# Swapping the PSUM pairs of the seven products, and emitting two activation sums later, in a hybrid decoder trunk

## The chip, the cores and the metric

The kernel runs on one core of one Trainium2 chip. The metric is the device time of one execution in microseconds: before the change 1286.51 us, the median of 3 runs from 1285.29 to 1288.07. The profile is one further execution. Engines are called by the names that the profile uses: PE multiplies matrices (PEld is its load of the stationary operand), DVE, ACT and POOL work element by element, SP issues most DMAs.

## The reference

A sequence of 512 tokens with 1024 channels passes two layers. Layer 0 mixes tokens by stick-breaking attention with 16 heads, layer 1 by a gated linear recurrence with 8 heads. Each mixer is followed by a squared-ReLU MLP of width 4096, with an RMSNorm in front:

```python
def squared_relu_mlp(h, w1, w2):
    a = jax.nn.relu(h @ w1)
    return (a * a) @ w2
...
    h = rmsnorm(x, norm_gains[layer, 1])
    x = x + squared_relu_mlp(h, mlp_w1[layer], mlp_w2[layer])
```

Everything is float32. The change lies in the MLP alone, which runs twice.

## The kernel before

Every matrix product is made of three multiplications of a reduced format: both operands are split into a high and a low part (`xh`, `xl` for activations, `wh`, `wl` for weights), and high times high, high times low and low times high are added up in PSUM.

The MLP (`mlp`) runs in four rounds, q = 0 to 3, each for 1024 of the 4096 hidden features.

- The first half of a round makes the hidden features from four slabs of `mlp_w1`, c = 0 to 3. Each slab gives two tiles, j = 0 and 1, by `gemm_w`: a chain of 24 matmuls, 8 groups of 3, into one PSUM bank. In each group the second and the third matmul are (low activations, `wh`) and (high activations, `wl`). DVE then makes `u` from the bank (ReLU times the norm's factor, line 866), and `Seven.take` squares it and forms sums and differences of the halves of the activations.
- The second half multiplies by `mlp_w2` with Strassen's seven products (`seven_products`). They are named n = 0 to 6: a11, s1, a12, s4, s2, s3, a22. Each has its own slab of weights and two chains, t = 0 and 1, of 12 matmuls. After each chain a function (`p1` to `p7`) adds the bank to the residual stream `xt` on DVE, by `back` (line 714), some by way of a tile `U`.

PSUM has eight banks of 128x512: a pair called `mm`, a pair called `z`, three called `tr` and one called `av`. A pair is used in turn. The tiles of the first half use `mm` (in round 0 the first two use `z`). The products take `mm` for even n and `z` for odd n, so the first product (a11) and the last (a22) use `mm`, as do the hidden features ahead of a11 and behind a22. A chain can begin only when the bank has been read by whoever used it last.

The weights come through `Weights`. One call of `next` hands out the slab that is ready and prepares the one after it: SP or POOL load the raw half slabs, ACT makes `wh` (line 266 for `mlp_w1`, line 301 for `mlp_w2`), DVE makes `wl` (lines 267 and 302). Each slab has two halves, so there are two ACT and two DVE instructions per slab. There are two buffers for `wh`, `wl` and for the raw tiles `wr` of `mlp_w1`. The sums and differences of weights are made by DMAs that add on arrival, and by an ACT sign flip on line 293; its first flip for the next round is issued as soon as the data of the next round have landed.

PE runs in the order of the program. The other engines run in an order that a scheduler makes at build time from the order of the program and its own estimate of when each input is ready; every engine then works through its list in order.

`Seven.take` handles features 0 to 7 of a round. For features 4 to 7 (k = 0 to 3 after `k -= 4`) it makes `a2`, `s31` and, by two DVE subtractions on lines 785 and 786 and one more split, `s42`. `s42` is read by products n = 3 and n = 4.

Of the kernel before, what the change touches and what calls it, by code (L numbers as in the profile page):

```python
# [13 lines left out]
ALU = mybir.AluOpType  # L14
# [45 lines left out]
def trunk(  # L60
# [17 lines left out]
    nc = tc.nc  # L78
# [13 lines left out]
    def sb(tag, shape=(P, S), dt=F32, name=None):  # L92
        pool = gp if tag in "PQ" else ap
        return pool.tile(list(shape), dt, tag=tag, bufs=BUFS[tag], name=name or tag)

    def ps(tag, shape=(P, S), name=None):
        return pp.tile(list(shape), F32, tag=tag, bufs=PB[tag], name=name or f"ps_{tag}")

    def f(t):
        return t.bitcast(F32)  # L100
# [78 lines left out]
    def gain(layer, j, kt):  # L179
# [15 lines left out]
        out=later[:, 3 * P :], in_=later[:, 3 * P :], pattern=[[-1, P]], compare_op=ALU.is_gt,  # L195
# [4 lines left out]
        out=before[:, P:], in_=before[:, P:], pattern=[[1, P]], compare_op=ALU.is_gt,  # L200
# [188 lines left out]
    def gemm_w(o, wsl, j, acts, toks=slice(0, S)):  # L389

        hi, lo = wsl
        c = slice(j * P, (j + 1) * P)
        n = len(acts)
        for k in range(n):
            ah, al = acts[k]
            mm(o, hi[:, k, c], ah[:, toks], k == 0, False)
            mm(o, hi[:, k, c], al[:, toks], False, False)
            mm(o, lo[:, k, c], ah[:, toks], False, k == n - 1)
            yield
# [313 lines left out]
    def back(h, t, p, op=ALU.add):  # L713
        nc.vector.tensor_tensor(out=xt[h][:, t, :], in0=xt[h][:, t, :], in1=p, op=op)  # L714

    def chain(o, wsl, acts):

        hi, lo = wsl
        n = len(acts)
        for k, (ah, al) in enumerate(acts):  # L720
            mm(o, ah, hi[:, k, :], k == 0, False)
            mm(o, ah, lo[:, k, :], False, False)
            mm(o, al, hi[:, k, :], False, k == n - 1)
            yield
# [17 lines left out]
    def two(wsl, norm):  # L742

        got = [ps("z"), ps("z")]
        hi, lo = wsl
        for n, (h, task) in enumerate(norm.turned):
            yield [task]
            for j in range(2):
                c = slice(j * P, (j + 1) * P)
                for k in range(4 * h, 4 * h + 4):  # L750
                    ah, al = norm.acts[k]
                    mm(got[j], hi[:, k, c], ah, n == 0 and k == 4 * h, False)
                    mm(got[j], hi[:, k, c], al, False, False)
                    mm(got[j], lo[:, k, c], ah, False, n == 1 and k == 4 * h + 3)
                    yield
        return got

    class Seven:
# [5 lines left out]
        def take(self, u):  # L764

            A, B = slice(0, S // 2), slice(S // 2, S)
            k = len(self.raw)
            if k < 4:
                raw = sb("AT" if k else "qT", name="raw_a")
                self.raw.append(raw)  # L770
                nc.scalar.activation(out=raw, in_=u, func=AF.Square)
                hl = sb("Q", dt=F32R, name="a11")
                self.a11.append((hl[:, A], hl[:, B]))
                nc.scalar.copy(hl[:, A], raw[:, A])
                nc.vector.tensor_tensor(out=hl[:, B], in0=raw[:, A], in1=f(hl[:, A]), op=ALU.subtract)
                nc.vector.tensor_tensor(out=raw[:, A], in0=raw[:, A], in1=raw[:, B], op=ALU.subtract)
                return
            k -= 4
            a, raw = sb("sn", name="a"), self.raw[k]
            self.raw.append(a)  # L780
            nc.scalar.activation(out=a, in_=u, func=AF.Square)
            nc.vector.tensor_tensor(out=raw[:, B], in0=raw[:, B], in1=a[:, B], op=ALU.add)
            self.a2.append(self.two_parts(a, "Q", "a2"))
            self.s31.append(self.two_parts(raw, "qT", "s31"))
            nc.vector.tensor_tensor(out=a[:, B], in0=a[:, B], in1=raw[:, A], op=ALU.subtract)
            nc.vector.tensor_tensor(out=a[:, A], in0=a[:, A], in1=a[:, B], op=ALU.subtract)
            self.s42.append(self.two_parts(a, "Q" if k < 2 else "qT", "s42"))

        def two_parts(self, src, tag, name):
            h, l = act_pair(tag, name)  # L790
# [9 lines left out]
            }[name]  # L800
            return [[blk(x, at + t) for x in pair] for pair in src]

    def seven_products(A, done):


        U = []

        def p1(t, p):
            U.append(sb("AT", name="U"))
            nc.scalar.copy(U[t], p)  # L810
            back(0, t, p)

        def p2(t, p):
            back(0, t, p)
            done(0, t)

        def p5(t, p):
            back(1, t, p, ALU.subtract)
            back(1, 2 + t, p, ALU.subtract)

        def p3(t, p):
            back(1, t, p)

        def p6(t, p):
            nc.vector.tensor_add(U[t], U[t], p)  # L825
            back(1, t, U[t])
            done(1, t)

        def p7(t, p):
            nc.vector.tensor_add(U[t], U[t], p)  # L830
            back(1, 2 + t, U[t])
            done(1, 2 + t)
            back(0, 2 + t, U[t])

        def p4(t, p):
            back(0, 2 + t, p, ALU.subtract)
            done(0, 2 + t)

        steps = [
            ("a11", p1), ("s1", p5), ("a12", p2), ("s4", p3), ("s2", p6), ("s3", p7), ("a22", p4),  # L840
        ]
        for n, (name, then) in enumerate(steps):
            wsl = weights.next()
            for t in range(2):
                p = ps("z" if n % 2 else "mm", name="ps_mm")
                yield from chain(p, wsl, A.part(name, t))
                then(t, p)

    def mlp(norm, nxt=None):
        task = line.spawn(norm.finish())  # L850
        rounds = FF // D
        for q in range(rounds):
            A = Seven()
            for c in range(4):
                wsl = weights.next()
                if q + c == 0:
                    early = yield from two(wsl, norm)
                    yield [task]
                for j in range(2):
                    if q + c == 0:  # L860
                        p = early[j]
                    else:
                        p = ps("mm")
                        yield from gemm_w(p, wsl, j, norm.acts)
                    u = sb("sq", name="u")
                    nc.vector.scalar_tensor_tensor(  # L866
                        out=u, in0=p, scalar=0.0, in1=norm.R, op0=ALU.max, op1=ALU.mult
                    )
                    A.take(u)

            def done(h, t):
                if q < rounds - 1:
                    return
                if nxt is None:
                    nc.sync.dma_start(
                        out=out[0, t * P : (t + 1) * P, h * S : (h + 1) * S], in_=xt[h][:, t, :]
                    )
                    return
                nxt.squares(h, t)
                if t == TT - 1:  # L880
                    nxt.turn(h, LAG["x7"] if h else LAG["x"])

            yield from seven_products(A, done)


    def hgrn(norm):
# [274 lines left out]
    def trunk_steps():  # L1161
        outs, heads = yield from attention(Norm(0, 0))
        norm = Norm(0, 1)
        yield from project(outs, [heads[:8], heads[8:]], norm)
        nxt = Norm(1, 0)
        yield from mlp(norm, nxt)
        line.width = 3
        outs, mixes = yield from hgrn(nxt)
        norm = Norm(1, 1)
        yield from project(outs, [mixes[:4], mixes[4:]], norm)  # L1170
        yield from mlp(norm)
# [7 lines left out]
    for c in range(4):  # L1179
        for j in range(2):  # L1180
            k = 2 * c + j
            nc.sync.dma_start(
                out=xt[k // 4][:, :, (k % 4) * P : (k % 4 + 1) * P],
                in_=x[0, :, k * P : (k + 1) * P].rearrange("(t p) c -> p t c", p=P),
            )
            if j == 0:
                i = 2 * (c % 2)
                nc.sync.dma_start(
                    out=start["raws"][c // 2][:, i : i + 2, :],
# [10 lines left out]
    with tc.manual_schedule(engines={mybir.EngineType.PE}):  # L1200
        p = ps("av", name="ps_w")
# [52 lines left out]
```

## Time and profile before

| | before |
|---|---|
| median of 3 runs | 1286.51 us |
| the profiled execution's own time | 1282.32 us |
| its span | 1280.6 us |
| PE busy | 1241.3 us, 97% |
| DVE busy | 955.4 us, 75% |
| ACT busy | 611.1 us, 48% |
| PE waiting for `xt` on DVE in front of `ps_mm` | 5.0 us, 7 times |

The span is the time from the first to the last instruction in the trace; 1.7 us of the execution lie outside it. Matmuls of 512 columns start 0.23 us apart when nothing holds them up, but each is drawn 0.39 us long, since the next one starts while it is still under way. So the idle time that a row gives in front of a matmul is about 0.16 us less than the delay of its start.

### The profile page before, as it was taken

How to read it: one execution, taken by the hardware profiler on the slowest of the kernel's cores; microseconds unless marked ns; L12 is line 12 of the kernel's file. 1: busy time of each engine (PE TensorE's matmuls, PEld its weight loads, DVE VectorE, ACT ScalarE, POOL GpSimd, SP SyncE). 2: the span in 40 equal slices, each digit the busy share in tenths (PEclk: the TensorE clock that was granted, in tenths of full speed). 3: DMA queues.
4: the chain of work that ended last, by engine and by line, in shares of the span. 5: the costliest groups of instructions: out<-in, count | busy, mean ns of one | idle time of the engine just before them, and what ended most of it. 6: DMA issues, size and time to landing. Idle time of an engine off the chain costs nothing. (4 is left out here: it accounts for less than half of the span.)

```text
span 1280.6 us, 17916 instructions
## 1 busy us (share of the span) xinstructions
PE 1241.3 (97%) x6817; PEld 1071.3 (84%) x6817; DVE 955.4 (75%) x1799; ACT 611.1 (48%) x991; POOL 148.4 (12%) x207
## 2 busy tenths in 40 slices
PE   7999999999999999999999999999999999999998
PEld 7999999788878878788788888888888788787787
DVE  4798787865875866768878888888667758667686
ACT  4555455544734645536532424333346436356272
POOL 1000001000110100201022222223000101002010
PEclk8999999999999999999999999999999999999999
DMA  5312125332293572954321212225431944828615
GB/s 162 116 34 67 42 72 136 100 100 81 66 241 120 108 222 66 202 159 87 94 83 46 87 53 80 64 85 136 144 99 47 242 138 88 229 78 180 181 34 131
DMA packets 104502, 144.23 MB, mean 113 GB/s; under 512 B 4856, under 2 KB 70560, under 8 KB 104416
## 3 DMA queue, kind: packets, MB, share of 16 engines
q1 hardware_dynamic: 91024, 109.22, 26.6%
q0 software_dynamic: 13392, 33.87, 14.9%
q8 instruction: 54, 0.88, 0.3%
q14 instruction: 32, 0.26, 0.1%
HBM read 124.19 MB, written 2.10 MB: 99 GB/s over the span
## 5 line engine op out<-in xcount | busy, mean ns | idle before, releaser
L154 PE MATMUL ps_mm<-xh,wh 128*128 128x512 f32 x592 | 232.7, 393 | 4.0 <-DVE xt L714 4.0
L154 PE MATMUL ps_mm<-xh,wl 128*128 128x512 f32 x592 | 230.5, 389 | 0.0
L154 PE MATMUL ps_mm<-xl,wh 128*128 128x512 f32 x592 | 230.4, 389 | 0.0
L266 ACT CAST wh<-wr 128x1024 fp32r<-128x1024 f32 x134 | 136.8, 1052 | 143.3 <-PE ps_mm L154 87.0
L267 DVE TENSOR_TENSOR wl<-wr,wh 128x1024 fp32r<-128x1024 f32 x134 | 163.5, 1233 | 34.2 <-ACT wh L266 33.9
L154 PE MATMUL ps_mm<-wh,xh 128*128 128x256 f32 x592 | 172.8, 292 | 0.0
L154 PE MATMUL ps_mm<-wl,xh 128*128 128x256 f32 x592 | 167.5, 283 | 2.3 <-DVE wl L540 2.3
L154 PE MATMUL ps_mm<-wh,xl 128*128 128x256 f32 x592 | 167.7, 283 | 0.0
L302 DVE TENSOR_TENSOR wl<-raw,wh 128x1024 fp32r<-128x1024 f32 x112 | 132.8, 1221 | 35.9 <-ACT wh L301 35.8
L154 PEld LDWEIGHTS ps_mm<-xh,wh 128*128 128x128 f32 x592 | 111.2, 188 | 28.8 <-issue 6.4
L301 ACT CAST wh<-raw 128x1024 fp32r<-128x1024 f32 x112 | 111.4, 1047 | 43.9 <-PE ps_mm L154 40.4
L154 PEld LDWEIGHTS ps_mm<-xh,wl 128*128 128x128 f32 x592 | 111.1, 188 | 23.3
L154 PEld LDWEIGHTS ps_mm<-xl,wh 128*128 128x128 f32 x592 | 111.2, 188 | 22.2
L714 DVE TENSOR_TENSOR xt<-xt,ps_mm 128x512 f32<-128x512 f32 x128 | 86.1, 683 | 47.2 <-PE ps_mm L154 47.1
L154 PEld LDWEIGHTS ps_mm<-wl,xh 128*128 128x128 f32 x592 | 113.4, 191 | 3.0 <-DVE wl L540 2.5
L154 PEld LDWEIGHTS ps_mm<-wh,xh 128*128 128x128 f32 x592 | 113.4, 192 | 0.5
L154 PEld LDWEIGHTS ps_mm<-wh,xl 128*128 128x128 f32 x592 | 113.3, 191 | 0.0
L317 POOL DMA_DIRECT2D raw<-in_mlp_w_dram x16 | 19.4, 1242 | 585.0 <-DVE wl L302 585.0
L866 DVE SCALAR_TENSOR_TENSOR u<-ps_mm,R 128x512 f32<-128x512 f32 x60 | 41.3, 689 | 47.8 <-PE ps_mm L154 47.8
L293 ACT ACTIVATE raw<-raw 128x1024 f32<-128x1024 f32 x48 | 50.8, 1058 | 36.5 <-DMA raw<-in_mlp_w_dram 35.6
L1028 DVE COPY_PREDICATED sc<-masks,ps_s 128x32 f32<-128x32 uint8 (+9 forms) x176 | 46.6, 299 | 13.0 <-PE ps_s L154 11.0
L154 PE MATMUL ps_mm<-wl,s31h 128*128 128x512 f32 x128 | 51.2, 400 | 4.1 <-DVE wl L302 4.1
(236 smaller groups left out, 2547.9 us busy)
## 6 DMA issues: line engine op xcount, KB each, us to landing
raw<-in_mlp_w_dram SPq DMA_DIRECT2D x64, 512.0 KB, 5.9
wr<-in_mlp_w_dram SPq DMA_DIRECT2D x64, 512.0 KB, 4.2
raw<-in_mlp_w_dram POOLq DMA_DIRECT2D x32, 512.0 KB, 6.2
raw<-raw POOLq DMA_DIRECT2D x32, 512.0 KB, 5.8
wr<-in_hg_w_in_dram SPq DMA_DIRECT2D x32, 512.0 KB, 3.8
wr<-in_sb_w_qkv_dram SPq DMA_DIRECT2D x22, 512.0 KB, 3.5
wr<-in_sb_w_o_dram SPq DMA_DIRECT2D x8, 512.0 KB, 3.9
wr<-in_hg_w_o_dram SPq DMA_DIRECT2D x8, 512.0 KB, 4.1
```

Source lines behind the costliest of these rows:

```text
L154: nc.tensor.matmul(o, lhsT=lhsT, rhs=rhs, start=start, stop=stop, **kw)
L266: nc.scalar.copy(hi[:, c, :], raw)
L267: nc.vector.tensor_tensor(out=lo[:, c, :], in0=raw, in1=f(hi[:, c, :]), op=ALU.subtract)
L293: nc.scalar.mul(b[at][a], b[at][a], -1.0)
L301: nc.scalar.copy(hi[:, c, :], b[at][a])
L302: nc.vector.tensor_tensor(out=lo[:, c, :], in0=b[at][a], in1=f(hi[:, c, :]), op=ALU.subtract)
L317: nc.gpsimd.dma_start(out=b[0, 1][a], in_=rows(1, 1, a), accum_op=ALU.add)
L714: nc.vector.tensor_tensor(out=xt[h][:, t, :], in0=xt[h][:, t, :], in1=p, op=op)
L866: nc.vector.scalar_tensor_tensor(out=u, in0=p, scalar=0.0, in1=norm.R, op0=ALU.max, op1=ALU.mult)
L1028: nc.vector.copy_predicated(out=o, mask=mask.rearrange("p (g w) -> p g w", g=g)[:, None].to_broadcast([P, 2, g, w]), data=data.rearrange(" ...
```

## The change

The products of a round take the pairs the other way round (`z` for even n, `mm` for odd n), except in the last round (q = 3) of each MLP, which stays as it was. And of the last feature (k = 3) the two subtractions and the split into `s42` are no longer emitted inside `take` but in `seven_products`, right behind the call that hands out the slab of n = 0 and prepares that of n = 1.

```diff
@@ -782,9 +782,16 @@
             self.s31.append(self.two_parts(raw, "qT", "s31"))
-            nc.vector.tensor_tensor(out=a[:, B], in0=a[:, B], in1=raw[:, A], op=ALU.subtract)
-            nc.vector.tensor_tensor(out=a[:, A], in0=a[:, A], in1=a[:, B], op=ALU.subtract)
-            self.s42.append(self.two_parts(a, "Q" if k < 2 else "qT", "s42"))
+
+            def s42():
+                nc.vector.tensor_tensor(out=a[:, B], in0=a[:, B], in1=raw[:, A], op=ALU.subtract)
+                nc.vector.tensor_tensor(out=a[:, A], in0=a[:, A], in1=a[:, B], op=ALU.subtract)
+                self.s42.append(self.two_parts(a, "Q" if k < 2 else "qT", "s42"))
+
+            if k < 3:
+                s42()
+            else:
+                self.rest = s42
...
-    def seven_products(A, done):
+    def seven_products(A, done, last):
...
             wsl = weights.next()
+            if n == 0:
+                A.rest()
             for t in range(2):
-                p = ps("z" if n % 2 else "mm", name="ps_mm")
+                p = ps("z" if (n + (not last)) % 2 else "mm", name="ps_mm")
                 yield from chain(p, wsl, A.part(name, t))
                 then(t, p)
...
-            yield from seven_products(A, done)
+            yield from seven_products(A, done, q == rounds - 1)
```

No engine gets another instruction, and none loses one. What differs on PE is which matmuls wait, and for whom. At the end of round 0 of layer 0 PE has, before the change, the last matmul of a22 and then the first group of slab c = 0 of round 1 (`ps_mm_4099` is the bank of a22, t = 1; `ps_mm_4127` that of c = 0, j = 0; `wh_4075` and `wl_4076` are that slab):

```order
L154 MATMUL ps_mm_4099<-wh_4037,a2l_3828 128x512
L154 MATMUL ps_mm_4127<-xh_3321,wh_4075 128x512 [waits DVE_49,Activation_49]
L154 MATMUL ps_mm_4127<-xl_3322,wh_4075 128x512
L154 MATMUL ps_mm_4127<-xh_3321,wl_4076 128x512
L154 MATMUL ps_mm_4127<-xh_3337,wh_4075 128x512
```

And after it:

```order
L154 MATMUL ps_mm_4099<-wh_4037,a2l_3828 128x512
L154 MATMUL ps_mm_4127<-xh_3321,wh_4075 128x512 [waits DVE_49,Activation_49]
L154 MATMUL ps_mm_4127<-xl_3322,wh_4075 128x512
L154 MATMUL ps_mm_4127<-xh_3321,wl_4076 128x512 [waits DVE_49]
L154 MATMUL ps_mm_4127<-xh_3337,wh_4075 128x512
```

The first matmul still waits for a DVE instruction, now the one that read the bank two products earlier; the third has a wait of its own for the low half of the weights, which the first one's wait used to cover. The fifth group's third matmul has had a wait for the second half of `wl` in both.

Further up in the same round PE goes from c = 3 to a11 (n = 0). Before, with `ps_mm_3797` the bank of c = 3, j = 1, and `ps_mm_3853` that of a11, t = 0:

```order
L154 MATMUL ps_mm_3797<-xh_3496,wl_3650 128x512
L154 MATMUL ps_mm_3853<-wh_3747,a11_3553 128x512 [waits DVE_49,Activation_49]
L154 MATMUL ps_mm_3853<-wl_3748,a11_3553 128x512
L154 MATMUL ps_mm_3853<-wh_3747,a11_3553 128x512
L154 MATMUL ps_mm_3853<-wh_3747,a11_3561 128x512
```

After:

```order
L154 MATMUL ps_mm_3797<-xh_3496,wl_3650 128x512
L154 MATMUL ps_mm_3853<-wh_3747,a11_3553 128x512 [waits Activation_49]
L154 MATMUL ps_mm_3853<-wl_3748,a11_3553 128x512 [waits DVE_49]
L154 MATMUL ps_mm_3853<-wh_3747,a11_3553 128x512
L154 MATMUL ps_mm_3853<-wh_3747,a11_3561 128x512
```

The first matmul of a11 no longer waits for DVE to have read a bank of c = 3; the wait for `wl` has moved to the matmul that reads it.

On DVE the place is where the second slab of the products (n = 1, `wl` from `raw_3403` and `raw_3405`) meets the sums of the last feature (`a_3824`, `raw_a_3639`). Before:

```order
L866 SCALAR_TENSOR_TENSOR u_3822<-ps_mm_3797,R_3532 128x512 [waits PE_49]
L302 TENSOR_TENSOR wl_3842<-raw_3403,wh_3841 128x1024 [waits DMASW1_49,Activation_49]
L302 TENSOR_TENSOR wl_3842<-raw_3405,wh_3841 128x1024 [waits DMASW2_49,Activation_49]
L782 TENSOR_TENSOR raw_a_3639<-raw_a_3639,a_3824 128x256 [waits Activation_49]
L714 TENSOR_TENSOR xt0_99<-xt0_99,ps_mm_3853 128x512 [waits Activation_49]
L792 TENSOR_TENSOR a2l_3828<-a_3824,a2h_3827 128x512
L792 TENSOR_TENSOR s31l_3832<-raw_a_3639,s31h_3831 128x512 [waits Activation_49]
L785 TENSOR_TENSOR a_3824<-a_3824,raw_a_3639 128x256 [waits DVE_49]
L786 TENSOR_TENSOR a_3824<-a_3824 128x256 [waits DVE_49]
```

After:

```order
L875 SCALAR_TENSOR_TENSOR u_3822<-ps_mm_3797,R_3532 128x512 [waits PE_49]
L302 TENSOR_TENSOR wl_3836<-raw_3403,wh_3835 128x1024 [waits DMASW1_49,Activation_49]
L302 TENSOR_TENSOR wl_3836<-raw_3405,wh_3835 128x1024 [waits DMASW2_49,Activation_49]
L782 TENSOR_TENSOR raw_a_3639<-raw_a_3639,a_3824 128x256 [waits Activation_49]
L714 TENSOR_TENSOR xt0_99<-xt0_99,ps_mm_3853 128x512 [waits Activation_49]
L799 TENSOR_TENSOR a2l_3828<-a_3824,a2h_3827 128x512
L799 TENSOR_TENSOR s31l_3832<-raw_a_3639,s31h_3831 128x512 [waits Activation_49]
L787 TENSOR_TENSOR a_3824<-a_3824,raw_a_3639 128x256 [waits DVE_49]
L788 TENSOR_TENSOR a_3824<-a_3824 128x256 [waits DVE_49]
```

Nothing moved: the scheduler had put the second slab ahead of these sums already. Only line and buffer numbers differ. The same holds for the whole lists of DVE, ACT, POOL and SP, with their waits; on PE no matmul changes its place, and only the waits shown, in each of the six rounds that are not last ones, are others.

## Rows read from the trace of the kernel before

**Rows 1.** The page: busy time by engine, the granted PE clock in 40 equal slices of the span, and the chain that ended last by engine and by line.

```profile
PE 1241.3 (97%) x6817; PEld 1071.3 (84%) x6817; DVE 955.4 (75%) x1799; ACT 611.1 (48%) x991; POOL 148.4 (12%) x207
...
PEclk8999999999999999999999999999999999999999
...
PE 19%; DMA 3%; DVE 2%; issue 1%; ACT 0%; ACTq 0%; DVEq 0%
PE ps_mm L154 19%; DMA raw<-in_mlp_w_dram 3%; DVE wl L302 1%; DVE xt L714 1%; DVE U L825 0%; PE ps_z L154 0%; ACT wh L301 0%; DVE U L830 0%; PE ps_bc L154 0%; DVE dg L493 0%; DVE wl L267 0%; ACT raw L293 0%; ACTq L301 0%; DVEq L302 0%; ACTq L293 0%
```

**Rows 2.** The waits of PE over the whole span: who waited for whom, us in total, times, longest.

```profile
PE ps_mm L154 <- DVE xt L714: 5.0, 7, 1.0
PE ps_mm L154 <- DVE wl L302: 4.1, 6, 0.8
...
PE ps_mm L154 <- ACT wh L301: 1.1, 3, 0.6
```

**Rows 3.** The page's groups of instructions: the first matmul form of `gemm_w`, with the idle time in front of it, and the DVE additions into `xt` (count, busy us, mean ns).

```profile
L154 PE MATMUL ps_mm<-xh,wh 128*128 128x512 f32 x592 | 232.7, 393 | 4.0 <-DVE xt L714 4.0
...
L714 DVE TENSOR_TENSOR xt<-xt,ps_mm 128x512 f32<-128x512 f32 x128 | 86.1, 683 | 47.2 <-PE ps_mm L154 47.1
```

**Rows 4.** The timeline of PE where round 1 of layer 0 ends and round 2 begins: start us, duration us, then what ran, and in brackets the idle time before it and who ended it.

```profile
465.99 0.39 PE L154 MATMUL ps_mm<-wl,a2h 128*128 128x512 f32 x1
466.22 0.39 PE L154 MATMUL ps_mm<-wh,a2l 128*128 128x512 f32 x1
467.28 0.47 PE L154 MATMUL ps_mm<-xh,wh 128*128 128x512 f32 x1 [0.67 <-DVE xt L714]
467.58 0.40 PE L154 MATMUL ps_mm<-xl,wh 128*128 128x512 f32 x1
467.82 0.40 PE L154 MATMUL ps_mm<-xh,wl 128*128 128x512 f32 x1
468.05 0.40 PE L154 MATMUL ps_mm<-xh,wh 128*128 128x512 f32 x1
```

**Rows 5.** The loads of the stationary operand (PEld) for the first and the third matmul of the same group.

```profile
467.25 0.19 PEld L154 LDWEIGHTS ps_mm<-xh,wh 128*128 128x128 f32 x1 [1.06 <-issue]
...
467.59 0.19 PEld L154 LDWEIGHTS ps_mm<-xh,wl 128*128 128x128 f32 x1
```

**Rows 6.** The timeline of DVE over the same boundary.

```profile
463.39 0.68 DVE L830 TENSOR_TENSOR U<-U,ps_mm 128x512 f32<-128x512 f32 x1
464.11 1.29 DVE L714 TENSOR_TENSOR xt<-xt,U 128x512 f32<-128x512 f32 x2
465.32 1.22 DVE L267 TENSOR_TENSOR wl<-wr,wh 128x1024 fp32r<-128x1024 f32 x1
466.45 0.68 DVE L714 TENSOR_TENSOR xt<-xt,ps_mm 128x512 f32<-128x512 f32 x1
467.05 1.22 DVE L267 TENSOR_TENSOR wl<-wr,wh 128x1024 fp32r<-128x1024 f32 x1
468.18 0.68 DVE L714 TENSOR_TENSOR xt<-xt,ps_mm 128x512 f32<-128x512 f32 x1
471.38 1.23 DVE L267 TENSOR_TENSOR wl<-wr,wh 128x1024 fp32r<-128x1024 f32 x1 [2.51 <-ACT wh L266]
474.02 1.22 DVE L267 TENSOR_TENSOR wl<-wr,wh 128x1024 fp32r<-128x1024 f32 x1 [1.41 <-ACT wh L266]
```

**Rows 7.** The timeline of PE at the other five ends of a round that is not a last one: the first matmul of the next round.

```profile
382.36 0.47 PE L154 MATMUL ps_mm<-xh,wh 128*128 128x512 f32 x1 [0.69 <-DVE xt L714]
...
551.13 0.47 PE L154 MATMUL ps_mm<-xh,wh 128*128 128x512 f32 x1 [0.67 <-DVE xt L714]
...
1025.95 0.47 PE L154 MATMUL ps_mm<-xh,wh 128*128 128x512 f32 x1 [0.69 <-DVE xt L714]
...
1110.62 0.47 PE L154 MATMUL ps_mm<-xh,wh 128*128 128x512 f32 x1 [0.65 <-DVE xt L714]
...
1194.46 0.47 PE L154 MATMUL ps_mm<-xh,wh 128*128 128x512 f32 x1 [0.67 <-DVE xt L714]
```

**Rows 8.** The timeline of PE inside c = 0, j = 0 of round 2: the second and the third matmul of the fifth group, of which the third waits for the second half of `wl`; and, below, the first matmul of c = 1.

```profile
470.35 0.39 PE L154 MATMUL ps_mm<-xl,wh 128*128 128x512 f32 x1
470.58 0.39 PE L154 MATMUL ps_mm<-xh,wl 128*128 128x512 f32 x1
...
478.28 0.39 PE L154 MATMUL ps_mm<-xh,wh 128*128 128x512 f32 x1
```

**Rows 9.** The timeline of PE at the start of product s3 (n = 5) of round 1 of layer 0, and that of ACT ahead of it.

```profile
454.29 0.51 PE L154 MATMUL ps_mm<-wh,s31h 128*128 128x512 f32 x1 [0.57 <-ACT wh L301]
455.55 0.50 PE L154 MATMUL ps_mm<-wl,s31h 128*128 128x512 f32 x1 [0.75 <-DVE wl L302]
455.89 0.39 PE L154 MATMUL ps_mm<-wh,s31l 128*128 128x512 f32 x1
...
442.69 2.01 ACT L301 CAST wh<-raw 128x1024 fp32r<-128x1024 f32 x2 [3.45 <-PE ps_mm L154]
449.66 1.06 ACT L293 ACTIVATE raw<-raw 128x1024 f32<-128x1024 f32 x1 [4.96 <-DMA raw<-in_mlp_w_dram]
452.24 1.06 ACT L293 ACTIVATE raw<-raw 128x1024 f32<-128x1024 f32 x1 [1.52 <-DMA raw<-in_mlp_w_dram]
453.20 3.87 ACT L301 CAST wh<-raw 128x1024 fp32r<-128x1024 f32 x4
```

## The prediction

> **What bounds the kernel now.** Read the page first [rows 1]. PE is busy for 1241.3 of 1280.6 us, and the chain that ended last is PE's, with a few per cent of DVE and DMA. DVE is busy for three quarters of the span. So a change can pay only by what PE waits, some 39 us in all. The granted clock is 9 tenths or more, its upper level of 2.4 GHz, in every slice but the first, so none of these short waits costs clock.
>
> Next the waits of PE [rows 2]. Three of them belong to the MLP rounds: 5.0 us in 7 waits for the addition into `xt`, 4.1 us in 6 for `wl` of line 302, 1.1 us in 3 for `wh` of line 301. The groups [rows 3] show that 4.0 of the 5.0 us stand in front of the first matmul of `gemm_w`, that is, where one round follows another. Two layers with four rounds have six such places. The timelines show all six [rows 4, 7], with idle times of 0.65 to 0.69 us, always ended by the addition on line 714.
>
> Rows 4 to 6 tell why. PE is through with a22 and wants the pair `mm` for c = 0 of the next round. That pair still holds a22. Its first bank was full a chain ago, but DVE works through a list: the last addition of s3, then half of the next slab's `wl`, and only at 466.45 the addition that reads the bank. It ends at 467.13, and PE goes on at 467.28.
>
> **The stall that goes.** Undisturbed matmuls start 0.23 us apart. Here the start of c = 0 comes 467.28 - 466.22 = 1.06 us after the last matmul of a22, so it is 0.83 us late (the 0.67 us of the row and the 0.16 us by which a matmul is drawn longer than its spacing). The next start comes after 0.30 instead of 0.23 us, another 0.07. Together 0.90 us per place. Over six places: 4.0 us of idle time [rows 3], 6 x 0.16 = 1.0 and 6 x 0.07 = 0.4 make 5.4 us.
>
> After the change a22 sits in `z`, and c = 0 takes the `mm` banks of s3. DVE read the second of them at 463.39 to 464.07 (line 830) and the first before it [rows 6], over 2 us before PE asks at 466.45. So the bank no longer holds PE up. The next user of `z` is a11 of the next round, four slabs later, or in a last round s1.
>
> **What is late next.** Three things must be ready when PE starts at 466.45 instead of 467.28.
> - `wh` of the slab: ACT has long cast it.
> - The first half of `wl`. The order shows that the third matmul now waits for it by itself. It would start at 466.45 + 2 x 0.23 = 466.91. DVE ends this half at 465.32 + 1.22 = 466.54, and from a DVE end to PE's next step it takes 0.12 us (467.13 to the load at 467.25) [rows 5, 6], so it is there at 466.66. It fits with 0.25 us to spare. The second half ends at 468.27; the fifteenth matmul needs it at 466.45 + 14 x 0.23 = 469.7.
> - The slab of c = 1. Its last half of `wl` ends at 474.02 + 1.22 = 475.24 [rows 6]. PE began c = 1 at 478.28 [rows 8] and would begin it at 477.4. Two microseconds of cover stay; were they gone, the whole gain of that place would go with them.
>
> A wait that is already fulfilled costs nothing: the third matmul of the fifth group carries one today and starts 0.23 us after its neighbour [rows 8].
>
> The load of the stationary operand runs ahead: for the third matmul it started at 467.59, 0.23 us before the matmul at 467.82 [rows 4, 5]. The Trainium skill (TensorE: Matmul & The Clock Gate, "Step-by-step: what each phase is for") has the rule: PE pulls loads of weights ahead of matmuls that are under way. By it the new wait bites one matmul earlier, at 466.68 against a half slab that is there at 466.66, and the spare time is nothing; the trace agrees on the order of the two.
>
> What such a near miss costs is bounded by [rows 9]: where PE did stop for `wl`, the next start came after 0.34 instead of 0.23 us. A load that starts 0.1 us late still lets its matmul start on time (0.03 us behind it at 467.28, rows 4, 5), so the bounds are nothing and 0.11 us at each of six places, 0.7 us in all. I take 0.2 us, nearer to nothing, because the half slab is there on time by the rows.
>
> **The other edits.** The transition from c = 3 to a11 loses a wait for DVE that did not hold PE up: the waits of PE have no row of `u` in front of `ps_mm` among the MLP's [rows 2]. Worth nothing; a gain is excluded by the missing row, and a loss since the pair `z` has been free since the round before. The moved sums of the last feature keep their places in every list: the scheduler had placed the second slab's split ahead of them. Worth nothing, both ways, unless the lists differ on the chip, which they cannot.
>
> **The sum.** 5.4 - 0.2 = 5.2 us less. The profiled execution would go from 1282.32 to 1277.1 us, its span from 1280.6 to 1275.4. The median of the runs is 4.2 us above that execution; I take the difference off the median: 1286.5 - 5.2 = 1281.3 us.
>
> **Rivals.**
> 1. *The time is given back at product s3.* In rounds 0 to 2 PE waits there, 0.57 and 0.75 us by the rows shown, for a slab whose cast stands on ACT behind the sign flips of line 293, and these wait for data that SP and DMA bring [rows 9]. If the landing at 452.24 hangs on something that does not come earlier with PE, the stop grows by as much as PE gained. That takes back the gain of the four places that are followed by a round with this stop (into q = 1 and q = 2 in both layers), and leaves the two into q = 3, whose rounds have no such stop (6 waits in 8 rounds, rows 2): 2 x 0.9 = 1.8 us, 1284.7 us. For it speaks that DMA holds 3% of the chain. Against it: the cast at 442.69 is released by PE giving back a `wh` buffer, and raw buffers come free by the DVE instruction behind such casts, so this whole train starts when PE is at the products of the same round and moves with it.
> 2. *Slower: the new wait covers too much.* If the third matmul's wait on DVE came true only with the second half of `wl`, at 468.27 + 0.12 = 468.39, it would start at 468.4 instead of today's 467.82, and lose 0.58 and 0.1 for starting up again, 0.7 us at six places: 4.1 us, 1290.6 us. It decides as soon as that count is reached later than 0.9 us behind the first half. Against it: the fifth group keeps a wait of its own for the second half.
> 3. *The change does not do what it says.* Something else that DVE makes at the same moment would hold PE until 467.3 anyway, and the time stays 1286.5 us. The only inputs of the first two matmuls are old activations and `wh`, so I see nothing that could.
>
> **How the numbers follow.** A measurement of this kernel can tell about 0.2%, 2.6 us, from no change. Forecast 0.82 (5.2 us, 0.4%: faster), rival 1 0.09 (within 0.2%), rival 3 0.05 (within), rival 2 0.04 (slower). One in ten of the forecast's share may be spoilt by the spread of the runs, which reaches 1.6 us above the median, but then half of rival 1 may look faster. So faster 0.83, same 0.13, slower 0.04. The forecast's own range is a gain of 4.7 to 5.4 us, and 1 to 2 us on either side for the runs' spread and for the stops at s3, which differ between rounds by several tenths. Rival 1's 1284.7 us is taken in, rivals 2 and 3 are left out: 1278.5 to 1285.0 us.
>
> **What would show it.** Right: the waits of PE for `xt` in front of `ps_mm` fall from 7 to 1 and from 5.0 to about 1.0 us; the first matmul of each round starts 0.23 us after the last of a22; the waits for line 302 and line 301 keep their size. Rival 1: these two grow from 5.2 us together to about 9. Rival 2: a new wait of PE for `wl` of line 267, some 1.5 us each, six times. A few tenths of that row would be the near miss that I priced at 0.2. Wrong altogether would be the forecast if the first matmul of a round still stood idle, whoever ended it, or if DVE's additions at the boundary came later than now because a product's bank is read in another order.

## The result, and the profile after

| | before | after |
|---|---|---|
| median, runs on the same chip (5 each) | 1286.23 us | 1277.82 us |
| lowest to highest of them | 1281.2 to 1288.07 | 1275.55 to 1280.56 |
| the profiled execution's own time | 1282.32 us | 1279.44 us |
| its span | 1280.6 us | 1277.7 us |

The ratio is 0.9943, 95% interval [0.9921, 0.9966]: faster by 0.6%. That is about 8 us by the medians, 7.3 by the ratio, where 5.2 had been forecast. The two profiled executions differ by 2.9 us only. Both distances need an explanation, and the traces give most of it.

The page of the changed kernel, with the lines that answer to [rows 1] and the first of [rows 3]:

```profile
PE 1241.9 (97%) x6817; PEld 1073.6 (84%) x6817; DVE 955.0 (75%) x1799; ACT 611.8 (48%) x991; POOL 148.5 (12%) x207
...
PE 21%; DMA 2%; DVE 1%; ACT 0%; issue 0%; ACTq 0%
...
L154 PE MATMUL ps_mm<-xh,wh 128*128 128x512 f32 x592 | 232.1, 392 | 0.0
```

No engine works less or more. What changed is the last number: the idle time in front of the first matmul form of `gemm_w` was 4.0 us [rows 3] and is 0.0. The waits of PE (total us, times, longest) say the same:

```profile
PE ps_mm L154 <- DVE wl L302: 3.7, 6, 0.8
...
PE ps_mm L154 <- ACT wh L301: 1.7, 3, 0.9
...
PE ps_mm L154 <- DVE xt L714: 1.4, 2, 1.0
```

The wait for the addition into `xt` fell from 5.0 us in 7 times to 1.4 in 2; the two waits at s3 together went from 5.2 to 5.4 us [rows 2]. No row for `wl` of line 267 in front of `ps_mm` has appeared.

The timeline of PE where round 1 of layer 0 ends, which answers to [rows 4]:

```profile
466.11 0.39 PE L154 MATMUL ps_mm<-wh,a2l 128*128 128x512 f32 x1
466.33 0.39 PE L154 MATMUL ps_mm<-xh,wh 128*128 128x512 f32 x1
466.56 0.39 PE L154 MATMUL ps_mm<-xl,wh 128*128 128x512 f32 x1
466.79 0.39 PE L154 MATMUL ps_mm<-xh,wl 128*128 128x512 f32 x1
```

The load of the stationary operand for the third of these matmuls [rows 5]:

```profile
466.56 0.19 PEld L154 LDWEIGHTS ps_mm<-xh,wl 128*128 128x128 f32 x1
```

And DVE over the same boundary [rows 6]:

```profile
463.97 1.29 DVE L714 TENSOR_TENSOR xt<-xt,U 128x512 f32<-128x512 f32 x2
465.18 1.22 DVE L267 TENSOR_TENSOR wl<-wr,wh 128x1024 fp32r<-128x1024 f32 x1
466.32 0.68 DVE L714 TENSOR_TENSOR xt<-xt,ps_mm 128x512 f32<-128x512 f32 x1
```

DVE does what it did, in the same order and as late: its addition for a22 begins at 466.32. But PE passes from a22 to c = 0 in 0.23 us (466.11 to 466.33) where it took 1.06. The half slab of `wl` ends at 465.18 + 1.22 = 466.40, and the load that needs it starts on time at 466.56. All six round ends look like this: from the last matmul of a22 to the first of c = 1 it takes 11.11 us at every one, and took 12.03 to 12.08. That is 0.92 to 0.97 us six times, 5.7 us.

Why then do the profiled executions differ by 2.9 us? The trace of after has two stretches in which TensorE ran at its lower level of 1.2 GHz at places where the trace of before has none. When the two traces are matched matmul by matmul, after loses 2.4 us at each of these two places. Before has such a stretch of its own in layer 0's attention, at 239.7 to 243.1, which after lacks; there after gains 1.0 us. It gains 5.7 us at the round ends and 0.9 us at the start and in small waits, and all this together makes the 2.9 us. One of the two stretches is at s3 of round 0 of layer 0. PE's rows there:

```profile
367.57 0.40 PE L154 MATMUL ps_mm<-wh,s42l 128*128 128x512 f32 x1
368.83 0.50 PE L154 MATMUL ps_mm<-wh,s31h 128*128 128x512 f32 x1 [0.86 <-ACT wh L301]
370.09 0.61 PE L154 MATMUL ps_mm<-wl,s31h 128*128 128x512 f32 x1 [0.76 <-DVE wl L302]
370.50 0.63 PE L154 MATMUL ps_mm<-wh,s31l 128*128 128x512 f32 x1
370.93 0.63 PE L154 MATMUL ps_mm<-wh,s31h 128*128 128x512 f32 x1
```

And three windows of the same trace (window, its length, busy time and count of PE, PEld, DVE, ACT and POOL, then the granted clock, DMA share, GB/s): ahead of the stops, behind them, and later. The last line is the stretch in the trace of before.

```profile
366.50:367.50 1.00, 1.00 (x6) 0.82 (x5) 0.00 (x0) 0.75 (x2) 0.67 (x1) 1.00 0.93 356
370.50:373.50 3.00, 3.00 (x9) 2.33 (x8) 2.93 (x5) 1.11 (x2) 0.00 (x0) 0.50 1.09 198
380.00:383.00 3.00, 3.00 (x15) 2.47 (x14) 3.00 (x4) 0.00 (x0) 0.00 (x0) 1.00 0.31 85
```

```profile
239.70:243.10 3.40, 3.40 (x13) 2.63 (x12) 3.10 (x6) 0.67 (x2) 0.00 (x0) 0.50 0.01 2
```

After two stops in a row the granted clock is 0.50 for some 3 us; matmuls start 0.43 us apart instead of 0.23, eight of them, which is 1.6 us lost on top of the stops. The second such stretch stands behind two stops between the layers, at 640. From the start of the last matmul on `s42` to that of the first of a22, with the 24 of s3 between, it takes 9.50 us here and 7.10 in the trace of before; undisturbed it takes 5.82. (This is the segment at s3 that is meant below.) So one profiled execution more or less says little about a difference of 5 us; the segments between fixed instructions do.

### The profile page after: what moved, and what is told of

It is laid out like the page before. It is cut to its first block, busy times and chain, and to the rows that moved or that the text cites. A ratio compares the mean times of both kernels' runs of the same rounds, so it can differ in the third digit from the quotient of the medians.

```text
span 1277.7 us, 17916 instructions
## 1 busy us (share of the span) xinstructions
PE 1241.9 (97%) x6817; PEld 1073.6 (84%) x6817; DVE 955.0 (75%) x1799; ACT 611.8 (48%) x991; POOL 148.5 (12%) x207
## 5 line engine op out<-in xcount | busy, mean ns | idle before, releaser
L302 DVE TENSOR_TENSOR wl<-raw,wh 128x1024 fp32r<-128x1024 f32 x112 | 132.8, 1221 | 36.2 <-ACT wh L301 36.1
```

What stands on the lines that cost most here:

```text
L302: nc.vector.tensor_tensor(out=lo[:, c, :], in0=b[at][a], in1=f(hi[:, c, :]), op=ALU.subtract)
```

## The experiments

The ratios are to the kernel before, from runs on the same chip, with the 95% interval.

| run | kernel | median us | ratio |
|---|---|---|---|
| e1 | before, pairs swapped | 1278.66 | 0.9958 [0.9942, 0.9975] |
| e2 | before, sums moved | 1283.77 | 0.9997 [0.9985, 1.0009] |
| e3 | before, one DVE instruction more ahead of the round end | 1287.48 | 1.0027 [1.0016, 1.0037] |
| e4 | after, the same instruction | 1281.54 | 0.9980 [0.9969, 0.9991] |
| e5 | after, a quarter of it | 1278.51 | 0.9957 [0.9942, 0.9972] |
| e6 | after, swapped in last rounds too | 1279.60 | 0.9964 [0.9951, 0.9977] |
| e7 | after, a sign flip on POOL | 1279.94 | 0.9966 [0.9954, 0.9979] |
| e8 | after, that flip on POOL from round 1 on | 1270.03 | 0.9889 [0.9874, 0.9904] |
| e9 | after, again | 1277.08 | 0.9940 [0.9928, 0.9953] |
| e10 | before, with the flip as in e8 | 1271.00 | 0.9909 [0.9892, 0.9927] |
| e11 | before, again | 1284.95 | 1.0007 [0.9996, 1.0018] |

**The two parts, one at a time.** e1 is the kernel before with

```diff
-                p = ps("z" if n % 2 else "mm", name="ps_mm")
+                p = ps("z" if (n + (not last)) % 2 else "mm", name="ps_mm")
```

> Only the pairs are swapped; the last feature's sums stay where they were in the code. Theory (the banks do it all, the moved sums nothing): the same time as the changed kernel, ratio to the kernel before 0.993 to 0.997; PE's wait for xt in front of ps_mm 1 to 1.5 us. Rival (the part of the 8.4 us gain above the 5.2 us forecast comes from the moved sums): ratio 0.996 to 0.998, about 3 us above the changed kernel. Second theory, on the spread: the runs of one kernel differ by the number of 3.41 us stretches at half the granted clock; two runs whose mean clock differs by 0.0013 (one stretch more) differ by 1.5 to 2.1 us, and among runs of equal clock this kernel is 5 to 6 us ahead of the kernel before.

e2 is the changed kernel with that line put back, so that only the moved sums remain.

> Only the last feature's sums are emitted later; the pairs stay as before. Theory: nothing moves in any engine's list, so the kernel before: ratio 0.998 to 1.002, and PE waits 5 us for xt in front of ps_mm, six times 0.65 to 0.7 at the ends of rounds. Rival (the moved sums bring some 3 us): ratio 0.997 to 0.998.

e1's round ends are those of after (11.11 us, six times), e2's those of before but for one. In the waits of PE of e2 the row stands again:

```profile
PE ps_mm L154 <- DVE xt L714: 4.7, 7, 1.0
```

The banks do all of it; the sums do nothing. The one exception in e2 is a round end of layer 1 (at 1113.84) with 0.23 us: 12 us ahead of it the clock had fallen, PE was slower by that, and DVE had caught up before PE asked for the bank. With the old pairs, a stretch at the lower clock is thus partly hidden by the stall it shortens.

Of e1's second theory one half held: at equal clock e1's runs are 5.4 us ahead of those of the kernel before. The other half did not: by a straight line through these 35 runs, 0.0013 of mean clock goes with some 0.8 us, not 1.5 to 2.1.

**Is it DVE's lateness that sets the price?** e3 adds, in rounds that are not last, one DVE instruction without use right behind the second chain of s3, to the kernel with the old pairs; e4 adds it to the changed kernel:

```diff
         def p7(t, p):
             nc.vector.tensor_add(U[t], U[t], p)
+            if t == 1 and not last:
+                nc.vector.tensor_tensor(out=later[:, :S], in0=U[t][:, :S], in1=later[:, :S], op=ALU.max)
             back(1, 2 + t, U[t])
```

> The kernel before, with one more DVE instruction of 0.69 us ahead of the last additions of s3 in the six rounds that are not last ones; it adds work and leaves nothing out. Theory (PE waits for the bank that the addition on line 714 frees): every stop at a round's end grows by 0.69 us, PE's wait for xt from 5.0 to 9.1 us, the time by 4.1 us, ratio about 1.003. Rival (something else holds PE at that place): no change of the stop.

> The changed kernel with the same 0.69 us DVE instruction at the same six places. Theory (the bank no longer binds, the low half of the slab binds next, and its wait sits on the load of the stationary operand): the half slab is there at 0.65 us after the load wants it, the third matmul starts 0.45 us late and the one behind it another 0.1; 0.55 us at six places, 3.3 us above the changed kernel, PE waits about 3 us for wl of line 267. Rival 1 (DVE at that place no longer matters to PE): as the changed kernel. Rival 2 (a late load delays its matmul in full): 4 us or more above the changed kernel.

e5 is e4 with `:P` (128 columns) in place of `:S` (512).

> The changed kernel with a DVE instruction of 128 columns (0.2 to 0.3 us) ahead of the last additions of s3 in the six rounds that are not last ones; it adds work and leaves nothing out. It uses up what the half slab of wl has to spare. Theory (a load that comes late by less than its lead of 0.23 us costs nothing): the load of the third matmul waits 0.1 to 0.2 us, its matmul starts at most 0.05 us late, ratio to the kernel before as for the changed kernel, 0.9945 to 0.9965, PE waits under 0.5 us in all for wl of line 267. Rival (the wait counts from the load on, so its delay is passed on): 0.2 to 0.3 us at each of six places, 1.5 us above the changed kernel.

In e3 the wait grows to

```profile
PE ps_mm L154 <- DVE xt L714: 9.0, 8, 1.3
```

and the round ends from 1.04 to 1.08 us to 1.64 to 1.66, by 0.59: the added instruction is drawn 0.69 us long, but the next DVE instruction starts 0.61 behind it. In e4 the bank is not what PE waits for. It is the third matmul, for the half slab of `wl`; first PE's rows, then the load's, then DVE's:

```profile
468.23 0.39 PE L154 MATMUL ps_mm<-xh,wh 128*128 128x512 f32 x1
468.46 0.39 PE L154 MATMUL ps_mm<-xl,wh 128*128 128x512 f32 x1
468.97 0.50 PE L154 MATMUL ps_mm<-xh,wl 128*128 128x512 f32 x1
```

```profile
468.97 0.19 PEld L154 LDWEIGHTS ps_mm<-xh,wl 128*128 128x128 f32 x1 [0.55 <-DVE wl L267]
```

```profile
465.88 0.69 DVE L839 TENSOR_TENSOR later<-U,later 128x512 f32<-128x512 f32 x1
...
467.70 1.22 DVE L267 TENSOR_TENSOR wl<-wr,wh 128x1024 fp32r<-128x1024 f32 x1
```

The idle time is in the load's row, and the matmul's shows none, since 0.39 of the 0.51 us from its neighbour's start count as busy: that the start comes 0.28 us late is the sign. DVE was late by 0.62 us (465.88 to 466.50, where its next instruction starts), the load by 0.51 (it belongs at 468.46, with the matmul ahead of its own), the matmul by 0.28. Five of six segments went from 11.11 to 11.51 or more, by 0.44 us in the mean: the 0.28 us and some 0.15 until starts are 0.23 us apart again. The sixth followed a stretch at the lower clock and lost nothing. In e5 DVE was late by 0.21 us, and the segments took 11.11 to 11.15. PE and its loads where round 1 of layer 0 ends:

```profile
469.25 0.39 PE L154 MATMUL ps_mm<-xl,wh 128*128 128x512 f32 x1
469.48 0.40 PE L154 MATMUL ps_mm<-xh,wl 128*128 128x512 f32 x1
...
469.38 0.19 PEld L154 LDWEIGHTS ps_mm<-xh,wl 128*128 128x128 f32 x1 [0.16 <-DVE wl L267]
```

The load is 0.13 us late and its matmul on time, and no segment lost more than 0.05 us. So the spare is 0.1 us at the load and 0.3 us at the matmul; what goes beyond the second costs PE time.

**The exception for last rounds.** e6 drops it:

```diff
-                p = ps("z" if (n + (not last)) % 2 else "mm", name="ps_mm")
+                p = ps("z" if (n + 1) % 2 else "mm", name="ps_mm")
```

> The pairs are swapped in the last rounds too. Theory (a pair binds only where the next user comes right behind a22): in layer 0 the first tiles of the recurrence take z right behind a22 of the last round and now wait for its additions, 0.5 to 1 us more in front of ps_z, once; in layer 1 nothing follows; 0 to 1 us above the changed kernel, ratio to the kernel before 0.995 to 0.998. Rival (the swap as such makes the products of a round quicker): 1 to 2 us below the changed kernel.

It lies with e1 within what the runs can tell. Between the layers no wait in front of `ps_z` appears: from the last matmul of s3 to the first tile in `z` it takes 7.43 us in e6 and 7.42 in e9, which is the changed kernel again. In these traces the exception is worth nothing, and the half to one microsecond that the theory allowed does not show.

**What is left at s3.** Of PE's waits in the MLP, those at s3 are left. The next runs move the flip that stands in ACT's list ahead of the casts of s3 [rows 9] to POOL:

```diff
-        def flip(at, plus):
+        def flip(at, plus, pool=False):
             for a in range(2):
-                nc.scalar.mul(b[at][a], b[at][a], -1.0)
+                if pool:
+                    nc.gpsimd.tensor_scalar(out=b[at][a], in0=b[at][a], scalar1=-1.0, scalar2=None, op0=ALU.mult)
+                else:
+                    nc.scalar.mul(b[at][a], b[at][a], -1.0)
...
-            flip((0, 1), lambda a: rows(0, 0, a))
+            flip((0, 1), lambda a: rows(0, 0, a), True)
```

> The changed kernel with the sign flip for the next round's t1 done by POOL instead of ACT, so that ACT's casts for product s3 no longer stand behind data of the next round. Theory (the stop at s3 is ACT's list, not the slab's own data): PE's waits for wl of line 302 and wh of line 301 fall from 5.4 us together to under 1 us, the six stops with their restarts, about 8 us by the trace of the changed kernel, go: ratio to the kernel before 0.988 to 0.992. Rival 1 (the slab's own adds by DMA land too late): the stops stay, ratio as for the changed kernel. Rival 2 (POOL's flips of 1024 columns slow DVE beside them): less than half of the gain, and DVE's instructions longer in the trace.

All stops at s3 went: each of the eight segments takes 5.82 us, and the waits for the products' `wh` and `wl` are gone from the list. Yet the time did not fall, since the flip for the first round of layer 1 now stands in POOL's list ahead of a product of the recurrence (`kk`). POOL, then PE:

```profile
883.93 3.33 POOL L294 TENSOR_SCALAR raw<-raw 128x1024 f32<-128x1024 f32 x1 [5.21 <-DMA raw<-in_mlp_w_dram]
887.24 0.61 POOL L1013 TENSOR_TENSOR kk<-kk,tot 128x256 f32<-128x256 f32 x1
```

```profile
889.76 0.90 PE L158 MATMUL kt<-ident,kk 128*128 128x128 f32 x3 [5.35 <-POOL kk L1013]
```

POOL waited 5.21 us for a transfer, worked 3.33 us, and PE stood for 5.35, with 6.8 us at the lower clock behind it (888.5 to 895.3). It is the same trouble moved to another engine: an instruction that waits for data from memory, ahead of one that PE needs. e8 keeps the flip of round 0 on ACT (`r0 > 0` in place of `True`), and e9 runs the changed kernel beside it.

> The changed kernel, with the first sign flip of a round's product weights on POOL instead of ACT, but only in rounds 1 to 3; in round 0 it stays on ACT, so that nothing long stands in POOL's list ahead of layer 1's recurrence. First theory: with the flip away from ACT's list the casts at s3 come in time, as they did with all flips on POOL, and the recurrence no longer waits for POOL. The stops at s3 of rounds 1 and 2 go (four of six; their segments of 24 matmuls come to 5.82 us instead of 6.3 to 7.5), those of round 0 stay (7.2 to 9.5 us), no stop of 5 us stands in the recurrence, and the half-clock stretches behind those stops go. That makes 4 to 5 us on top of the banks' gain: ratio to the kernel before 0.990 to 0.993, about 1273 to 1276 us. Second theory: POOL and DVE slow each other down, so that DVE's work comes late elsewhere; then the ratio stays at 0.994 to 0.998, and PE shows other waits for DVE of 3 us or more. Neither expects more than 0.998.

> The changed kernel once more, as it is, on the same chip as the one above. First theory: the banks' gain of 5 to 6 us is all there is, and the first comparison's 8.4 us held spread of the kernel before, whose runs went up to 1288: ratio 0.9945 to 0.9970. Second theory: the change is worth 8 us, and the runs with parts of it were short of it: ratio 0.9920 to 0.9940.

e8 gained more than either theory said: 15 us on the kernel before. The expectation had misplaced the flips: the one for round q + 1 stands in ACT's list during round q, so all six stops at s3 went, not four. The profiled executions of e8 and e9 (spans 1266.8 and 1275.1 us) differ by 8.3 us, and the six segments at s3 hold 7.75 of it (42.67 us against 6 x 5.82). e9 lies on the edge between its two theories.

**Do the two gains add up?** e10 is the kernel before, with the old pairs, and the flip as in e8; e11 is the kernel before.

> The kernel before, pairs unchanged, with the sign flips of rounds 1 to 3 on POOL. First theory: the bank stalls at the round ends and the stops at s3 are two separate costs that add up. Then the stops at s3 go here too (all segments 5.82 us; what the flip did on top of the changed kernel was 7 us), the six stalls at the round ends stay (starts 1.0 to 1.1 us apart, waits of PE for the addition into xt 4.5 to 5.0 us in 7), and the ratio to the kernel before is 0.993 to 0.9955. Second theory: the two cover each other in part, since PE arrives later at a round's end when it was stopped at s3, so that one costs more once the other is gone: then the round ends grow beyond 1.1 us (waits above 6 us) or the ratio is 0.9955 to 0.998.

> The kernel before as it is, for a second trace of it: its only profiled execution took 1282.3 us, and its runs since then 1283.5 to 1288. First theory: that execution is a quick one, and an ordinary one is longer where PE is stopped anyway (the start, s3, half-clock stretches), while the six round ends keep 1.0 to 1.1 us: then this trace, if it takes 1284 us or more, shows the extra 2 to 4 us in those places, and the change is worth 5.5 to 6 us by its own mechanism. Second theory: the round ends themselves are longer in an ordinary execution, 1.3 us or more, and the change is worth the 8 us that the medians differ by. Ratio to itself 0.9985 to 1.0015.

Neither of e10's theories foresaw what it shows: the round-end stalls go too, with the old pairs. Four of six ends take 0.23 us, two take 0.51 and 0.56. DVE in the kernel before, from further up than [rows 6]:

```profile
448.22 0.69 DVE L714 TENSOR_TENSOR xt<-xt,ps_mm 128x512 f32<-128x512 f32 x1 [1.48 <-PE ps_mm L154]
454.26 2.36 DVE L302 TENSOR_TENSOR wl<-raw,wh 128x1024 fp32r<-128x1024 f32 x2 [5.36 <-ACT wh L301]
456.54 0.68 DVE L825 TENSOR_TENSOR U<-U,ps_mm 128x512 f32<-128x512 f32 x1
```

And in e10, the same place, down to the addition that reads a22's first bank:

```profile
446.00 3.20 DVE L305 TENSOR_TENSOR wl<-raw,wh 128x1024 fp32r<-128x1024 f32 x2 [0.40 <-ACT wh L304]
449.12 0.67 DVE L828 TENSOR_TENSOR U<-U,ps_mm 128x512 f32<-128x512 f32 x1
...
459.11 1.22 DVE L267 TENSOR_TENSOR wl<-wr,wh 128x1024 fp32r<-128x1024 f32 x1
460.25 0.68 DVE L717 TENSOR_TENSOR xt<-xt,ps_mm 128x512 f32<-128x512 f32 x1
```

PE in e10 at s3's first read of that slab's `wl`, and at the round's end:

```profile
450.48 0.40 PE L154 MATMUL ps_mm<-wl,s31h 128*128 128x512 f32 x1
...
461.10 0.39 PE L154 MATMUL ps_mm<-wh,a2l 128*128 128x512 f32 x1
461.33 0.39 PE L154 MATMUL ps_mm<-xh,wh 128*128 128x512 f32 x1
```

The lists of DVE are the same. In the kernel before, DVE stands idle for 5.36 us, for the cast of line 301 that waits behind the flip, and the flip for its transfer [rows 9]. From 454.26 on it has no idle time of more than 0.04 us up to the addition that ends at 467.13. PE resumes at s3 on the same event, the first half of this `wl` (455.55, [rows 9]). From there both work without a pause: PE for the other 47 matmuls of s3 and a22, DVE for a list that takes some 0.8 us longer. That is why the six idle times at the round ends were alike within 0.04 us [rows 4, 7] although the stops at s3 were not: both engines started together, and the difference of their work was left over. In e10 DVE starts 4.48 us before PE's first matmul that reads the slab's `wl` (446.00 and 450.48), where it was 1.29 us in the kernel before (454.26 and 455.55); it ends the addition at 460.93, and PE begins c = 0 at 461.33 on time.

The two ends that keep a part of the stall are those where POOL's second flip fell on DVE's last split of the products' weights, which then takes 4.15 instead of 2.35 us. At the end of round 0 of layer 0 (DVE, POOL, PE):

```profile
369.18 4.15 DVE L305 TENSOR_TENSOR wl<-raw,wh 128x1024 fp32r<-128x1024 f32 x2
...
369.57 3.29 POOL L294 TENSOR_SCALAR raw<-raw 128x1024 f32<-128x1024 f32 x1
...
379.06 0.47 PE L154 MATMUL ps_mm<-xh,wh 128*128 128x512 f32 x1 [0.17 <-DVE xt L717]
```

The list of groups on the page has it in one line. DVE's split of the products' weights, in the kernel before and in e10 (idle time last):

```profile
L302 DVE TENSOR_TENSOR wl<-raw,wh 128x1024 fp32r<-128x1024 f32 x112 | 132.8, 1221 | 35.9 <-ACT wh L301 35.8
```

```profile
L305 DVE TENSOR_TENSOR wl<-raw,wh 128x1024 fp32r<-128x1024 f32 x112 | 139.9, 1284 | 9.5 <-ACT wh L304 9.3
```

So the flip, standing on ACT until its transfer lands, cost the kernel before both stalls, and the swap of the banks cured the second without touching its root. With the flip moved, the swap is worth 0.45 + 0.40 = 0.85 us by the segments of e10 against those of e8 (11.56 and 11.51 against 11.11); the medians differ by 1.0 us, on different chips, which the intervals do not tell from nothing.

e11's profiled execution took 1288.76 us, 6.4 more than the first of the same kernel. Its round ends take 1.04 to 1.08 us, but for one of 0.23 behind a stretch at the lower clock. The difference lies at the start (2 us), around the stops between the layers (2.7 us) and at s3 of layer 1 (2 us, of which 0.9 came back at that round end). That is the first theory: the mechanism of the change is worth 5.7 us a run, and executions differ by several us elsewhere.

## Why the prediction was right, and where not

- **The stall that goes**: right in place, cause at hand and size. Priced at 0.90 us per place, measured 0.92 to 0.97; six places, 5.7 us for 5.4.
- **The third matmul's new wait**: right that it fits. The spare was put at 0.25 us for the matmul and at nothing for the load; e4 and e5 have 0.3 and 0.1. From DVE's end to the load it takes 0.05 us (468.92 to 468.97 in e4), not the 0.12 that were taken from the bank's wait. The price taken, 0.2 us, was 0: the load is not late at all, and if it were, it may be late by a part of its lead before its matmul is, as one row of [rows 4, 5] had shown and e5 confirms.
- **The slab of c = 1**: PE begins it at 466.11 + 11.11 = 477.22 and the slab is ready at 475.0. Right.
- **The moved sums**: worth nothing, as e2 has it.
- **Rival 1** (given back at s3) fell: the segments at s3 are 6.3 to 7.5 us after and 6.6 to 7.7 before, apart from the one with the clock. **Rival 2** and **rival 3** fell with the rows at 466.
- **The waits of PE**: expected one left for `xt`, 1.0 us; there are two, 1.4. The second (0.47 us, in front of `wh,oh` at 244.40) is in layer 0's output product, outside the change; in before PE ran at the lower clock there and came later by itself.
- **The sum**: the profiled execution was to go to 1277.1 us and went to 1279.44; that of e9 took 1276.85. The median was to be 1281.3 and was 1277.82. That is 0.7 us below the stated range, 1278.5 to 1285.0; only the ratio, 0.9943 x 1286.51 = 1279.2 us, lies in it. The term that was mis-sized is the way from one profile to the medians, a difference of 4.2 us that was carried over unchanged: the profiled execution of after is 1.6 us above its median. Three comparisons give gains of 8.4, 5.3 (e1) and 8.0 us (e9), where the traces hold 5.7. The medians of the kernel before alone go from 1283.4 to 1286.2 us in the five comparisons. What makes the other 0 to 3 us was not settled; runs of one kernel lie up to 7 us apart, and the lower clock explains a part of that.
- **The chances**: nine tenths of 0.82 and half of 0.09 make 0.78 for faster, not the 0.83 that was stated.
- **"None of these short waits costs clock"** was wrong as a statement on the kernel. The 40 slices are 32 us each and hide a stretch of 3 us, as they did the one at 239.7 in before. The stops at s3 and between the layers do cost clock in some executions, 1.6 us and more at a time.
- **"DVE works through a list"** stopped one step early. It is why the bank was read late, but not why DVE was behind. The row of ACT waiting for a transfer was in [rows 9], used for rival 1 alone; followed back, it gives both stalls one root. By the segments it is worth 7.8 us at s3 (in the trace of before, 42.77 against 6 x 5.82) and 5.7 - 0.85 at the round ends, 12.7 us together; e10's median is 12.4 us ahead.

## What to carry to other kernels

When stalls of one size come back at the same place of every round while other waits vary, look for an event on which both engines started together. Here the stall was the difference of their work since then, and its root was what delayed that event. Before another bank or buffer is given to a late engine, follow its idle time back: here DVE's 35.9 us in front of one group, on an engine that was idle a quarter of the time, led over ACT's list to a transfer. And an instruction that waits for a transfer should stand in no in-order list ahead of work for the bottleneck, on ACT or, as e7 shows, on POOL. These are lessons from one kernel; no run here tries them on another.

## What the runs showed of the hardware

- Two stops of about 1 us with a single matmul between them were followed, in some executions, by 3 us at a granted clock of 0.50 (370.50 to 373.50 in after). In the ten traces that have stops at s3 this came seven times, where the first of the two starts came 1.17 to 1.35 us after the one ahead of it and the second 1.26; where the first came after 1.06 us or less, it did not come.
- POOL took 3.25 us in the mean for the sign flip of 128x1024 f32 in place (12 in e8), ACT 1.06 us for the same. Beside it two DVE splits took 3.20 or 4.15 instead of 2.36 us (e10); the mean of all 112 rose from 1221 to 1284 ns. DVE lost 0.8 to 1.8 us beside a flip of some 3.3 us, so it was not stopped for the whole of it.
- DVE instructions drawn 0.69 us long start 0.61 us apart, so that the start, not the drawn length, is what an added one costs (0.59 us in e3).
